# A streaming encoder layer on one core: token rows loaded three at a time and at an earlier gate, and convolution taps ordered behind softmax minima

## The chip, the cores and the metric

The kernel runs on one core of one Trainium2 chip. The metric is the device time of one execution in microseconds (us): 3044.03 us as the median of three runs of the kernel before. The engines of the core work in parallel and in order, each on its own queue: the matmul engine (PE, with its weight loads shown as PEld), the vector engine (DVE), the scalar engine (ACT), GpSimd (POOL), and SyncE (SP), which here issues the DMA transfers. They wait for one another by semaphores.

## The reference

One layer of a streaming encoder, in float32, for a prompt of 2048 tokens and a sample of 64 tokens (2112 in all), model width 1024:

- `h = rms_norm(x, norm1_g) * (1 + sc1) + sh1`, with scales and shifts from a small product of the condition `c`;
- one input projection `z = h @ w_in`, whose columns are a convolution pair (2 x 512), q, k, v (512 each) and two gates (1024 each);
- convolution branch: `u = glu_a * sigmoid(glu_b)`, a causal depthwise convolution of width 31 over the tokens, a LayerNorm over the 512 channels, swish, and a product with `w_conv_out`;
- attention branch: eight heads of 64, q and k normalised, each chunk of 64 tokens reads itself and the eight chunks before, a learned bias by distance, softmax, a product with v and with `w_attn_out`;
- the two are gated, added, projected by `w_o` and added to x; then a second RMS norm and a SwiGLU feed-forward layer of width 2816.

The outputs are the two token arrays and the new convolution, key and value states.

## The kernel before

**Stages.** The first phase (to about 1223 us of the profiled span) computes the input projection, the convolution and the attention in four token blocks: block 0 has the 64 sample tokens and 512 prompt tokens (576 columns), blocks 1 to 3 have 512 each. For each block the stages run in the order q, 0, k, 1, v, 2, 3, g: q, k and v are the attention's products, 0 to 3 are the four 128-channel tiles of the convolution pair, and g is the sixteen gate tiles of 128 columns. The second phase does the merge, the output projection and the feed-forward layer. Every product is made of three matmuls (`mm3`: the high part of the tokens `hh` by the high part of the weights `whi`, `hl` by `whi`, `hh` by `wlo`), so in the profile `ps<-hh,whi`, `ps<-hl,whi` and `ps<-hh,wlo` follow one another. In block 0 the weights are split into `whi` and `wlo` on the way (`wlo<-wst,whi` on DVE or POOL).

**What sets the order.** The program emits the big products in stage order, and between them work from *lanes* of generators: `norm_lane` (token tiles of the next block), `work` (rows of q and k), `attn` (attention heads), `tail` (LayerNorm after the convolution) and `conv` (the convolution's taps, in bursts of four). An object `Stream` adds up an estimated load for each engine; a lane hands on its next piece when the estimated time has come and the engines' estimated backlog is under the lane's room. What is emitted is then given by the framework's scheduler to each engine's queue; the emission order and the dependencies decide, and the queue is fixed when the program is built.

**Token rows.** At gate 11 (`NORM_G`) of a block's g stage the generators of the next block's four prompt tiles are put on `norm_lane`, two at work at a time. Each (`norm_tile`) loads its 128 x 1024 tokens (`x_t`, 512 KB, three buffers), goes on when 8 us of estimated PE time have passed (`X_LAG`), squares and sums them on ACT (`junk<-x_t`), scales them on DVE (`x_t<-x_t,r`), transposes them on PE (`pt<-ident,x_t`, two groups of four), applies scale and shift on DVE (`h<-pt,A,B`) and splits the result into `hh` (ACT) and `hl` (DVE), which the block's products read.

**Taps.** `glu` makes u, the convolution's input for 128 channels, and `convolve` applies the 31 taps to it on DVE: the first is a multiply and add with the bias (`y<-u,wd,cols`), the other thirty are `y<-u,wd,y`, each reading the y of the one before. In block 0 they are 606 columns wide, in the others 512. When a block's taps are done, POOL adds the four channel tiles into `s`, and PE multiplies that by a matrix of ones for the channel means (`pm<-s,ones`): in block 0 first for the 64 sample columns, then for 512.

**Attention.** For each head and each 128 queries PE forms the scores (`sc<-kk,q`), DVE adds the bias and takes a minimum along the row in one custom instruction (`pr<-sc,bias`, called the minimum here; the bias and scale are signed so that it stands for the maximum), ACT takes the exponentials, DVE a reciprocal of the sum (`sm<-sm`). Then PE transposes (`ptp<-ident,pr`), ACT and DVE split (`ph`, `pl<-ptp,ph`) and PE multiplies by the values (`po<-ph,vv`, `po<-pl,vv`). Two score buffers are used in turn; a further score product waits for the minimum of the one two before it, or, in block 0, where two products share a buffer, of the one before. The instruction of the last minimum is kept in `now["least"]`, which nothing reads before the change.

Of the kernel before, what the change touches and what calls it, by code (L numbers as in the profile page):

```python
# [11 lines left out]
ALU = mybir.AluOpType  # L12
# [4 lines left out]
P = 128  # L17
# [15 lines left out]
QB = 512  # L33
# [13 lines left out]
X_LAG = 8000.0  # L47
# [5 lines left out]
SIDE_G = 10  # L53
SPLIT_G = 2
NORM_G = 11
NORM_W = 2
SCORE_ROOM = {"dve": 2500}
TURN_NS = 600.0
# [12 lines left out]
def halves(lo, hi):  # L71
    n = hi - lo
    if n <= 512:
        return [(lo, hi)]
    mid = lo + n // 2
    return [(lo, mid), (mid, hi)]
# [511 lines left out]
def streaming_layer(ctx: ExitStack, tc: tile.TileContext, I, O):  # L588
    nc = tc.nc
    stream = Stream()  # L590
    pe, dve, act, gps = (
        Meter(e, n, stream) for e, n in ((nc.tensor, "pe"), (nc.vector, "dve"), (nc.scalar, "act"), (nc.gpsimd, "pool"))
    )
# [10 lines left out]
    def rows(prompt, sample, t, n):  # L604
        return prompt[t - SMP : t - SMP + n] if t >= SMP else sample[t : t + n]
# [32 lines left out]
    wd = const.tile([P, 4, TAPS], F32, name="wd")  # L638
# [59 lines left out]
    def rsqrt_mean(pool, ssq, n, width, count):  # L698
        t = pool.tile([P, 8], F32, tag="rs_t", bufs=4)
        r = pool.tile([P, 8], F32, tag="rs_r", bufs=4)  # L700
        dve.tensor_scalar(t[:n, :width], ssq, 1.0 / count, EPS, ALU.mult, ALU.add)
        stream.after("pool", "dve")
        gps.tensor_tensor(r[:n, :width], t[:n, :width], mhalf[:n, :width], ALU.pow)
        return r[:n, :width]
# [30 lines left out]
    def temp(name, shape=(P, 512)):  # L735
        return wk.tile(list(shape), F32, tag="t", name=name, bufs=NT)
# [345 lines left out]
    def load_x(t, n, pool, tag, bufs):  # L1082
        x_t = pool.tile([P, D], F32, tag=tag, name="x_t", bufs=bufs)
        nc.sync.dma_start(x_t[:n], rows(x_p, x_s, t, n))
        return x_t

    def square(x_t, n):
# [4 lines left out]
        dve.tensor_tensor(ssq[:n, 0:1], ssq[:n, 0:1], ssq[:n, 1:2], ALU.add)  # L1092
        return rsqrt_mean(wk, ssq[:n, 0:1], n, 1, D)

    def norm_tile(lo, t, free):

        c = slice(t - lo, t - lo + P)
        x_t = load_x(t, P, wa, "x", 3)
        yield stream.load["pe"] + X_LAG
        r = square(x_t, P)  # L1100
        yield stream.when("pool")
        dve.tensor_scalar(x_t, x_t, r, None, ALU.mult)
        yield stream.when("dve") + PE_LAG
        for g in range(2):
            pt = ps_g.tile([P, 4, P], F32, tag="gp", name="pt")
            h = temp("h32", (P, 4, P))
            for k in range(4):
                pe.transpose(pt[:, k], x_t[:, (4 * g + k) * P : (4 * g + k + 1) * P], ident)
            stream.after("dve", "pe")
            for k in range(4):  # L1110
                kk = 4 * g + k
                dve.tensor_scalar(h[:, k], pt[:, k], A1[:, kk, 0:1], B1[:, kk, 0:1], ALU.mult, ALU.add)
            yield stream.when("dve")
            yield lambda: free["columns"] >= c.stop
            f = slice(4 * g, 4 * g + 4)
            act.activation(hh[:, f, c], h, AF.Copy)
            yield stream.when("act")
            dve.tensor_tensor(hl[:, f, c], h, hh[:, f, c].bitcast(F32), ALU.subtract)
# [35 lines left out]
    def kts(t, a=0, b=KT):  # L1154
        return [t[:, k] for k in range(a, b)]
# [29 lines left out]

    now = {"scored": -1, "finished": -1, "bias": None}

    def convolve(u, y, ct, b):
        w = UW if b == 0 else HIST + QB
        n = w - HIST  # L1190
        states = [(cs_s, HIST + SMP)] if b == 0 else [(cs_p, w)] if b == len(PBLOCKS) - 1 else []
        if states:
            yield stream.when("dve") + TURN_LAG
        for rows_, e in states:
            pt = ps_g.tile([P, 512], F32, tag="gp", name="pt")
            pe.transpose(pt[:HIST, :P], u[:, e - HIST : e], ident)
            s = wa.tile([HIST, P], F32, tag="cc", name="cc", bufs=2)
            dve.tensor_scalar(s, pt[:HIST, :P], 0.5, None, ALU.mult)
            stream.at(stream.when("dve"), lambda s=s, rows_=rows_: nc.sync.dma_start(rows_[:, ct * P : (ct + 1) * P], s))
            yield  # L1200
        gps.tensor_copy(hist[:, ct], u[:, w - HIST : w])
        dve.tensor_scalar(y[:, ct, :n], u[:, :n], wd[:, ct, 0:1], bdw[:, ct : ct + 1], ALU.mult, ALU.add)
        for k in range(1, TAPS):
            dve.scalar_tensor_tensor(y[:, ct, :n], u[:, k : k + n], wd[:, ct, k : k + 1], y[:, ct, :n], ALU.mult, ALU.add)
            yield

    def conv_norm(y, c0, n, t0):
# [57 lines left out]
    def gates(b, free):  # L1265

        o = PBLOCKS[b][0]
        w = PBLOCKS[b][1] - o

        def part(g, ws, c0, c1):  # L1270
            ps = columns(*ws, kts(hh), kts(hl), c0, c1)
            t = temp("gate")
            stream.after("act", "pe")
            act.activation(t[:, : c1 - c0], ps[:, : c1 - c0], AF.Tanh, scale=0.5)
            nc.scalar.dma_start(g_d[g // 8, g % 8, :, o + c0 : o + c1], t[:, : c1 - c0])

        def pair(g):
            ws = [W.get(("in", 2560 + g * P, h)) for h in range(2)]
            return [[[w[l][:, k, e * P : e * P + P] for w in ws for k in range(4)] for l in range(2)] for e in range(2)]

        n = 16 - SPLIT_G if b + 1 < len(PBLOCKS) else 16
        for g in range(0, n, 2):
            for e, ws in enumerate(pair(g)):
                for c in halves(0, w):
                    part(g + e, ws, *c)
                if e:
                    W.done()
                    W.done()
                yield g + e
        rest = [ws for g in range(n, 16, 2) for ws in pair(g)]  # L1290
        for c0, c1 in ((0, w // 2), (w // 2, w)):
            for i, ws in enumerate(rest):
                part(n + i, ws, c0, c1)
                if c1 == w and i % 2:
                    W.done()
                    W.done()
            free["columns"] = c1
# [205 lines left out]

    norm_lane, work = Lane({}, wide=NORM_W), Lane({}, wide=3)
    attn = Lane(ATTN, ATTN_NS, wide=2)
# [6 lines left out]
    wa = side.enter_context(tc.tile_pool(name="wa", bufs=1, side="right"))  # L1512
# [11 lines left out]
    for b, stage in ORDER:  # L1524
        lo, hi = PBLOCKS[b]
        if stage == "q":
            free, ahead = {"columns": 0}, {}
            if b + 1 < len(PBLOCKS):
                ahead = {t: norm_tile(hi, t, free) for t, _ in token_tiles(*PBLOCKS[b + 1])}
        if stage == "q" and b == 0:  # L1530
            pass
        elif stage in ("q", "k", "v"):
            qkv(b, "qkv".index(stage), norms)
            if stage == "v":

                def heads(b=b):
                    work.drain()
                    stream.flush()
                    attention(b)
                    if b == 3:  # L1540
                        attn.burst, attn.spacing = 2, 0.0

                stream.at(stream.load["pe"] + HEADS_NS, heads)
        elif stage == "g":
            for g in gates(b, free):
                if g == NORM_G:
                    for gen in ahead.values():
                        norm_lane.add(gen)
                if g == SIDE_G and b == len(PBLOCKS) - 1:
                    work.drain()  # L1550
                    conv.drain()
                    stream.flush()
                    side.close()
                    wc = ctx.enter_context(tc.tile_pool(name="wc", bufs=1, side="right"))
                    cs = tile_chunks(*CBLOCKS[0])[0]
                    src = load_mixed(*cs, 0)
                    first_gates = gate_columns(*cs, 0)
            norms = ahead
        else:
            if b == 0 and stage == 1:  # L1560
                bias_rows()
            if stage == 0:
                conv.drain()
                tail.drain()
                y = wk.tile([P, 4, YW], F32, tag="y", name="y")
            conv.add(convolve(glu(b, stage), y, stage, b))
            if stage == 3:
                if b == 0:
                    tail.add(conv_norm(y, 0, SMP, 0))
                    tail.add(conv_norm(y, SMP + HIST, QB, SMP))  # L1570
                else:
                    tail.add(conv_norm(y, 0, QB, lo))
        for _ in range(MODS.get((b, stage), 0)):
            next(mods)
# [541 lines left out]
```

## Time and profile before

| | us |
|---|---|
| median of three runs (3043.26 to 3046.47) | 3044.03 |
| the profiled execution | 3045.71 |
| its span, first to last instruction | 3043.9 |
| PE busy in the span | 2932.8 |
| DVE, ACT, POOL busy | 1996.2, 1321.8, 984.2 |
| mean granted PE clock | 0.985 |

All lines of the profile are of one execution. An instruction line begins with its start in us from the span's start and its duration (of a group of equal ones the whole), then engine, line, operation, out<-in, shape and count; the brackets hold the idle time of the engine ahead of it and what ended it. All compute instructions are issued through one wrapper, so they carry one line number (L103 before, L104 after the change): they are told apart by the names of tiles and by shapes. A line of a stretch gives its bounds and, for each engine, busy time and number of instructions.

### The profile page before, as it was taken

To read this page: it belongs to the slowest core of one execution; us is meant where nothing else is said; L and a number is where in the kernel's file an instruction comes from. 1 tells how busy PE (TensorE), PEld (TensorE's weight loads), DVE (VectorE), ACT (ScalarE), POOL (GpSimd) and SP (SyncE) were. 2 spreads that over 40 slices of the span, in tenths; PEclk is the share of its full clock that TensorE was granted. 3 is DMA by queue.
4 is the path that set the end of the run, shared out by engine and by line. 5 is a ranking of instruction groups with operands and counts; after the bars stand their busy time and mean duration, and the time that the engine had idled before them with its cause. 6 is when DMAs were issued, how large, how long until landed. Compare 5 with 4: busy or idle time off the path is not lost. (4 is left out here: it accounts for less than half of the span.)

```text
span 3043.9 us, 44749 instructions
## 1 busy us (share of the span) xinstructions
PE 2932.8 (96%) x16259; PEld 2609.7 (86%) x16259; DVE 1996.2 (66%) x3595; ACT 1321.8 (43%) x2371; POOL 984.2 (32%) x617
## 2 busy tenths in 40 slices
PE   7989898999999999989999999999999999999998
PEld 4889776887888888878989889999999898999997
DVE  5896687667956895566666755655666756366567
ACT  3334542563365257463444425534444244333332
POOL 1200120101011102345677433247767341333331
PEclk9999998999999999999999999999999999999999
DMA  9788798877997788886444786455556965355544
GB/s 304 261 278 285 254 298 296 273 246 264 299 289 222 267 270 267 257 278 216 148 144 143 233 283 206 159 164 190 184 194 202 340 213 191 118 167 174 166 161 176
DMA packets 487018, 690.97 MB, mean 227 GB/s; under 512 B 38420, under 2 KB 316808, under 8 KB 486797
## 3 DMA queue, kind: packets, MB, share of 16 engines
q1 hardware_dynamic: 474517, 670.72, 67.2%
q10 hardware_dynamic: 12280, 17.39, 1.6%
q8 instruction: 128, 2.10, 0.3%
q14 instruction: 93, 0.76, 0.1%
HBM read 503.79 MB, written 184.19 MB: 226 GB/s over the span
## 5 line engine op out<-in xcount | busy, mean ns | idle before, releaser
L103 POOL TENSOR_TENSOR wlo<-wst,whi 128x1024 fp32r<-128x1024 f32 (+1 forms) x180 | 401.7, 2238 | 497.6 <-ACT whi L103 452.2
L103 PE MATMUL ps<-t,whi 128*128 128x384 f32 (+1 forms) x2112 | 507.4, 325 | 10.9 <-DVE t L103 5.2
L103 PE MATMUL pd<-whi,hid 128*128 128x512 f32 (+1 forms) x1400 | 450.6, 392 | 3.3 <-DVE acc L103 3.3
L103 ACT ACTIVATE whi<-wst 128x1024 fp32r<-128x1024 f32 (+1 forms) x273 | 266.1, 979 | 356.7 <-PE ps L103 123.4
L103 PE MATMUL ps<-b,whi 128*128 128x384 f32 (+1 forms) x1584 | 381.1, 326 | 11.6 <-DVE pw L103 4.0
L103 PEld LDWEIGHTS ps<-t,whi 128*128 128x128 f32 x2112 | 371.8, 190 | 19.2 <-DVE t L103 6.2
L103 DVE SCALAR_TENSOR_TENSOR y<-u,wd,y 128x512 f32<-128x512 f32 (+1 forms) x480 | 369.2, 773 | 8.2
L103 PE MATMUL ps<-hh,whi 128*128 128x512 f32 (+2 forms) x992 | 364.5, 367 | 1.0 <-DMA whi<-w_din_h 0.8
L103 PE MATMUL ps<-hl,whi 128*128 128x512 f32 (+2 forms) x992 | 346.9, 350 | 0.0
L103 PE MATMUL ps<-hh,wlo 128*128 128x512 f32 (+2 forms) x992 | 346.9, 350 | 0.0
L103 DVE TENSOR_TENSOR acc<-acc,pd 128x512 f32<-128x512 f32 (+1 forms) x440 | 290.7, 684 | 80.5 <-PE pd L103 76.7
L103 PE MATMUL ps<-t,wlo 128*128 128x384 f32 (+1 forms) x1056 | 341.6, 324 | 0.0
L103 PEld LDWEIGHTS pd<-whi,hid 128*128 128x128 f32 (+1 forms) x1400 | 258.4, 185 | 64.4 <-DVE acc L103 6.8
L103 PEld LDWEIGHTS ps<-b,whi 128*128 128x128 f32 x1584 | 277.9, 189 | 14.9 <-DVE pw L103 4.3
L103 PE MATMUL pd<-wlo,hid 128*128 128x512 f32 (+1 forms) x700 | 274.1, 392 | 0.0
L103 PE MATMUL ps<-b,wlo 128*128 128x384 f32 (+1 forms) x792 | 257.4, 325 | 0.0
L103 ACT ACTIVATE pr<-pr,sm 128x640 f32<-128x640 f32 (+3 forms) x272 | 200.1, 747 | 128.1 <-DVE sm L103 126.2
L103 POOL TENSOR_TENSOR r<-t,mhalf 128x1 f32<-128x1 f32 (+3 forms) x68 | 82.2, 1211 | 412.8 <-DVE t L103 369.1
L103 PEld LDWEIGHTS ps<-hh,wlo 128*128 128x128 f32 x992 | 188.2, 190 | 22.5 <-issue 0.4
L103 POOL TENSOR_TENSOR wlo<-wup,whi 128x1024 fp32r<-128x1024 f32 (+1 forms) x64 | 138.2, 2161 | 212.5 <-ACT whi L103 196.7
L103 PEld LDWEIGHTS ps<-hh,whi 128*128 128x128 f32 x992 | 189.1, 191 | 20.0 <-issue 2.7
L103 PEld LDWEIGHTS ps<-hl,whi 128*128 128x128 f32 x992 | 189.1, 191 | 15.5 <-issue 1.7
(215 smaller groups left out, 5719.6 us busy)
## 6 DMA issues: line engine op xcount, KB each, us to landing
whi<-w_din_h SPq DMA_DIRECT2D x72, 512.0 KB, 4.1
wlo<-w_din_l SPq DMA_DIRECT2D x72, 512.0 KB, 7.1
wst<-sum_d SPq DMA_DIRECT2D x131, 256.0 KB, 2.9
wmod<-in_w_ada SPq DMA_DIRECT2D x48, 512.0 KB, 7.2
sum_d<-ws SPq DMA_DIRECT2D x88, 256.0 KB, 2.5
wst<-in_w_ffn_in SPq DMA_DIRECT2D x85, 256.0 KB, 3.5
wst<-in_w_in SPq DMA_DIRECT2D x40, 512.0 KB, 7.4
wst<-in_w_ffn_in SPq DMA_DIRECT2D x37, 512.0 KB, 5.5
```

The lines of the kernel that those rows point to most:

```text
L103: return f(*args, **kw)
```

## The change

Two things are edited.

1. **Token rows.** A small function `ask` loads a tile's rows once and remembers when it may be used. At gate 3 (`ROWS_G`) of a block's g stage the first three tiles of the next block are asked for together; at gate 11 the generators start as before. The fourth tile, which needs a buffer of the three to be free, is asked for from inside the first tile's generator, after its second group of transposes.
2. **Taps.** In blocks 0 and 1 (`b < 2`) a tap that is emitted after a softmax minimum, the first since that minimum, is issued under `tc.issue_after(minimum)`: the scheduler may not put it ahead of that minimum in DVE's queue. No semaphore is added, since both are on one engine. The later taps of the same tile follow, since each reads the y of the one before.

```diff
+ROWS_G = 3
...
+    asked = {}
+
+    def ask(t):
+
+        if t not in asked:
+            asked[t] = load_x(t, P, wa, "x", 3), stream.load["pe"] + X_LAG
+
     def norm_tile(lo, t, free):
 
         c = slice(t - lo, t - lo + P)
-        x_t = load_x(t, P, wa, "x", 3)
-        yield stream.load["pe"] + X_LAG
+        ask(t)
+        x_t, landed = asked.pop(t)
+        yield landed
...
                 pe.transpose(pt[:, k], x_t[:, (4 * g + k) * P : (4 * g + k + 1) * P], ident)
+            if g and t + 3 * P < lo + QB:
+                ask(t + 3 * P)
...
+    def behind(one):
+
+        return tc.issue_after(one.ins) if one is not None else nullcontext()
+
...
         for k in range(1, TAPS):
-            dve.scalar_tensor_tensor(y[:, ct, :n], u[:, k : k + n], wd[:, ct, k : k + 1], y[:, ct, :n], ALU.mult, ALU.add)
+            with behind(now.pop("least", None) if b < 2 else None):
+                dve.scalar_tensor_tensor(y[:, ct, :n], u[:, k : k + n], wd[:, ct, k : k + 1], y[:, ct, :n], ALU.mult, ALU.add)
...
             for g in gates(b, free):
+                if g == ROWS_G:
+                    for t in list(ahead)[:3]:
+                        ask(t)
                 if g == NORM_G:
```

The rows below are those of the engines' queues as built (operation, out<-in, shape, count); ISA rows are the minimum and the read of its result.

DVE's queue in block 1, from the last u of the convolution to the four minima of the first head. Before:

```order
L103 SCALAR_TENSOR_TENSOR u<-tb,ps 128x512
L103 TENSOR_SCALAR y<-u,wd,cols 128x512
L103 COPY R<-pa 128x256
L103 SCALAR_TENSOR_TENSOR y<-u,wd,y 128x512 x4
L103 TENSOR_TENSOR A_173<-pa,cols 128x2x2x2
L103 SCALAR_TENSOR_TENSOR y<-u,wd,y 128x512
L103 TENSOR_TENSOR A_173<-A_173,cols 128x2x2x2
L103 SCALAR_TENSOR_TENSOR y<-u,wd,y 128x512 x15
L103 ISA pr,sm<-sc,bias 128x640
```

And now:

```order
L104 SCALAR_TENSOR_TENSOR u<-tb,ps 128x512
L104 TENSOR_SCALAR y<-u,wd,cols 128x512
L104 COPY R<-pa 128x256
L104 TENSOR_TENSOR A_173<-pa,cols 128x2x2x2
L104 TENSOR_TENSOR A_173<-A_173,cols 128x2x2x2
L104 ISA pr,sm<-sc,bias 128x640
L104 ISA sm 128x1
L104 RECIPROCAL sm<-sm 128x1
L104 ISA pr,sm<-sc,bias 128x640
```

Twenty taps (4, 1 and 15) stood between the u and the first minimum; none does now. In block 0 the corresponding rows are seven taps before and three now, and counted from the program's start 72 and 63.

DVE's queue in block 0, at the head whose last scores (64x320, the sample's) come just before the channel sum of the sample's columns. Before:

```order
L103 TENSOR_TENSOR pl<-ptp,ph 128x512
L103 ISA pr,sm<-sc,bias 64x320
L103 ISA sm 64x1
L103 TENSOR_TENSOR pl<-ptp,ph 128x384
L103 TENSOR_TENSOR pl<-ptp,ph 128x256
L103 TENSOR_TENSOR y<-y,pm 128x64 x4
```

And now:

```order
L104 ISA pr,sm<-sc,bias 64x320
L104 ISA sm 64x1
L104 SCALAR_TENSOR_TENSOR y<-u,wd,y 128x606
L104 TENSOR_TENSOR pl<-ptp,ph 128x256
L104 SCALAR_TENSOR_TENSOR y<-u,wd,y 128x606
L104 RECIPROCAL sm<-sm 64x1
L104 TENSOR_TENSOR wlo<-wst,whi 128x1024
L104 SCALAR_TENSOR_TENSOR y<-u,wd,y 128x606
L104 TENSOR_TENSOR wlo<-wst,whi 128x1024
L104 SCALAR_TENSOR_TENSOR y<-u,wd,y 128x606 x4
L104 TENSOR_TENSOR y<-y,pm 128x64 x4
```

Block 0's last seven taps now stand behind this minimum; before, all taps of block 0 were issued ahead of it. On PE, the product `pm<-s,ones 128x64` stands six `ps` and six `po` products after these scores.

PE's queue in block 3 at its first head (`q_10842`). Before, the first two of four score products:

```order
L103 MATMUL sc<-kk,q_10842 128x320 x4
L103 MATMUL ps<-hh,whi 128x512
L103 MATMUL ps<-hl,whi 128x512
L103 MATMUL ps<-hh,wlo 128x512
L103 MATMUL ps<-hh,whi 128x512
L103 MATMUL ps<-hl,whi 128x512
L103 MATMUL ps<-hh,wlo 128x512
L103 MATMUL sc<-kk,q_10842 128x320 x4
```

And now:

```order
L104 MATMUL ps<-hh,whi 128x512
L104 MATMUL ps<-hl,whi 128x512
L104 MATMUL ps<-hh,wlo 128x512
L104 MATMUL sc<-kk,q_10842 128x320 x16
L104 MATMUL ptp<-ident,pr 128x128 x2
```

The four score products stand in one run, with no other product between them, though the diff names neither block 3 nor the scores. On SP the token rows of block 1, which were two single loads and two later ones, are now one row of three (`DMA x_t<-in_x_prompt 128x1024 x3`) 35 places earlier in the queue, and a single load.

## The prediction

> **What bounds the kernel now.** I read the engines' shares first, then the idle stretches of the matmul engine (PE) in order of time with what ended each, then, at each of them, the vector engine (DVE) and the scalar engine (ACT) at the same moment, and last the granted clock of those stretches. The first line is the page's, the others are of the view by stretches (us; PE, PEld, DVE, ACT and POOL busy; granted clock; DMA share; GB/s).
>
> ```profile
> PE 2932.8 (96%) x16259; PEld 2609.7 (86%) x16259; DVE 1996.2 (66%) x3595; ACT 1321.8 (43%) x2371; POOL 984.2 (32%) x617
> ...
> 189.30:202.95 13.65, 7.96 (x27) 6.29 (x28) 12.22 (x25) 4.43 (x12) 0.00 (x0) 0.50 0.34 120
> 359.97:370.20 10.23, 7.32 (x19) 4.84 (x20) 6.54 (x20) 6.08 (x12) 3.74 (x3) 0.50 1.05 280
> 496.50:513.57 17.07, 7.11 (x23) 5.69 (x24) 15.00 (x29) 6.11 (x12) 0.00 (x0) 0.50 0.54 193
> 950.48:953.88 3.40, 1.77 (x7) 1.19 (x8) 3.34 (x10) 0.63 (x1) 1.18 (x1) 1.00 0.20 50
> 953.89:957.29 3.40, 3.40 (x10) 2.64 (x9) 2.99 (x8) 1.55 (x3) 0.27 (x1) 0.50 0.00 0
> 957.31:960.70 3.39, 3.39 (x22) 2.86 (x21) 1.98 (x3) 2.07 (x4) 1.35 (x1) 1.00 0.00 0
> ```
>
> PE is busy for 2932.8 of 3043.9 us, so only its idle time (111 us) and its half-speed time can be won. Three of the worst places are the ones that the change touches. A wait costs twice: in 950.48 to 953.88 PE was idle for 1.63 of 3.40 us, and the next 3.40 us, though full, ran at clock 0.50; after it the clock is 1.00 again. So I charge half of PE's busy time in a half-clock stretch: 7.96/2 = 4.0, 7.32/2 = 3.7 and 7.11/2 = 3.6 us. The waits (start, length; in brackets the idle time before and what ended it):
>
> ```profile
> 188.43 0.41 PE L103 MATMUL sc<-kk,q 128*128 128x128 f32 x2 [2.10 <-DMA kk<-k_d]
> 194.21 0.80 PE L103 MATMUL sc<-kk,q 128*128 128x256 f32 x2 [5.37 <-DVE sm L103]
> 355.73 0.47 PE L103 MATMUL po<-ph,vv 128*128 128x512 f32 x1 [1.28 <-DMA vv<-v_d]
> 360.04 1.97 PE L103 MATMUL pt<-ident,x_t 128*128 128x128 f32 x8 [3.61 <-DVE x_t L103]
> 365.62 0.79 PE L103 MATMUL ps<-whi,hh 128*128 128x512 f32 x1 [2.33 <-ACT hh L103]
> 504.61 1.43 PE L103 MATMUL sc<-kk,q 128*128 128x320 f32 x4 [10.18 <-DVE sm L103]
> 506.97 1.44 PE L103 MATMUL sc<-kk,q 128*128 128x320 f32 x4 [0.93 <-DVE sm L103]
> ```
>
> At 194.21 and 504.61 scores wait for DVE's minimum of the scores before. What DVE did until then (first a stretch: its busy time, the granted clock, DMA share, GB/s):
>
> ```profile
> 150.00:200.00 50.00, 48.09 (x71) 0.89 0.80 268
> ...
> 187.78 6.16 DVE L103 SCALAR_TENSOR_TENSOR y<-u,wd,y 128x606 f32<-128x606 f32 x7
> 193.86 0.28 DVE L103 CUSTOM_DVE_ANT_0 pr<-sc,bias 128x128 f32<-128x128 f32 x1
> ...
> 492.04 11.78 DVE L103 SCALAR_TENSOR_TENSOR y<-u,wd,y 128x512 f32<-128x512 f32 x15
> 503.73 0.82 DVE L103 CUSTOM_DVE_ANT_0 pr<-sc,bias 128x640 f32<-128x640 f32 x1
> ```
>
> Seven taps at 0.88 us (6.16/7) and fifteen at 0.785 (11.78/15) stood ahead of the minimum, and DVE was busy for 48.09 of the 50 us around the first head, so a tap less anywhere ahead of it counts in full. At 360.04 the cause is a late load:
>
> ```profile
> 351.25 0.50 SPq L1084 DMA_DIRECT2D x_t<-in_x_prompt  x1
> 353.10 0.70 SPq L1084 DMA_DIRECT2D x_t<-in_x_prompt  x1
> ...
> 356.86 0.63 ACT L103 ACTIVATE junk<-x_t 128x512 f32<-128x512 f32 x1 [2.48 <-DMA x_t<-in_x_prompt]
> 361.66 0.63 ACT L103 ACTIVATE junk<-x_t 128x512 f32<-128x512 f32 x1 [3.46 <-DMA x_t<-in_x_prompt]
> ```
>
> The third and fourth token tiles are asked for at 351 and 353 us, and ACT's squares of them wait at 356.86 and 361.66.
>
> **Gains.** First head of block 0: in the whole of DVE's order nine taps fewer stand ahead of the first minimum (63 instead of 72). Nine times 0.88 is 7.9 us, more than the wait of 5.37; what remains is the minimum itself, about 0.4. Gain 5.0. The wait of 2.10 for kk stays, and with what follows it is more idle time than the 1.63 us above, so one half-clock stretch of 3.4 us stays too (1.5 of the 4.0 us, the short waits between the four score products taking most of the rest). I take 6 us, 5 to 7.5.
>
> First head of block 1: twenty taps fewer ahead of the minimum, 20 x 0.785 = 15.7 us, more than the 10.18. Of the wait about 0.9 (minimum and its read) stays, and the two waits of 0.9 behind it, since two score buffers alternate with a minimum of 0.82. So 9.3 is won and nearly all the 3.6 of half clock; 1 off because the displaced taps meet the head's later work. I take 12, 10 to 13.5.
>
> Token rows, block 0 to 1: with three tiles in place by the fourth gate, the waits 1.28, 3.61 and 2.33 go with their half clock: 7.2 + 3.7 = 10.9. The fourth tile is still loaded inside the first tile's norm, and the transposes' chain through DVE and ACT (about 3 us) stands at another place among the products; 1 us off. I take 10, 8 to 12. The other blocks show no such row and get nothing. The three loads are 1.5 MB; at the 277 GB/s of the row below they take 5.7 us of the queues, ahead of weight slabs and the next heads' rows. I cost this at nothing: the same bytes are only moved, the DMA engines are 0.83 busy there, and weights are asked for ahead of use. Without that cover it is the third rival.
>
> **Losses.** The displaced taps return later, one behind each minimum, each holding up DVE's queue. First the rows for DVE's cover in block 0, then those at the place where its taps are needed (the sum for LayerNorm, pm).
>
> ```profile
> 250.00:290.00 40.00, 38.94 (x283) 37.23 (x282) 20.97 (x57) 22.49 (x54) 0.45 (x2) 1.00 0.83 277
> ...
> 256.41 1.21 DVE L103 TENSOR_TENSOR wlo<-wst,whi 128x1024 fp32r<-128x1024 f32 x1
> 257.61 1.72 DVE L103 SCALAR_TENSOR_TENSOR y<-u,wd,y 128x606 f32<-128x606 f32 x2
> 259.47 0.30 POOL L103 TENSOR_TENSOR s<-s,y 128x64 f32<-128x64 f32 x1 [33.78 <-DVE y L103]
> ...
> 286.00 0.30 PE L103 MATMUL ps<-hl,whi 128*128 128x288 f32 x1
> 286.13 0.29 PE L103 MATMUL ps<-hh,wlo 128*128 128x288 f32 x1
> 287.10 0.45 PE L103 MATMUL sc<-kk,q 128*64 128x320 f32 x2
> 287.57 0.69 DVE L103 TENSOR_TENSOR pl<-ptp,ph 128x512 fp32r<-128x512 f32 x1 [5.67 <-ACT ph L103]
> 288.18 0.47 DVE L103 CUSTOM_DVE_ANT_0 pr<-sc,bias 64x320 f32<-64x320 f32 x1
> 288.34 0.33 PE L103 MATMUL pm<-s,ones 128*128 128x64 f32 x2
> 290.56 0.39 PE L103 MATMUL po<-ph,vv 128*128 128x512 f32 x1
> 290.79 0.39 PE L103 MATMUL po<-pl,vv 128*128 128x512 f32 x1
> ```
>
> Before, the last tap ends at 259.4 and pm runs unhindered at 288.34: 29 us of slack, while DVE is about half busy (20.97 of 40). In the changed order seven taps, two wlo and one pl of 256 columns stand between the minimum of the 64x320 scores and the end of the taps: 7 x 0.86 + 2 x 1.21 + 0.4 (0.69 for 512) + 0.47 for the minimum = 9.3 us, then POOL's add, 0.30. PE has only six products of 288 columns (0.13 apart by 286.00 and 286.13) and six po between those scores and pm: 6 x 0.13 + 1.0 (0.23 apart for 512 columns, less for the shorter ones) = 1.8 us. PE waits 9.6 - 1.8 = 7.8. Idle that long, it then runs at half clock until a full stretch is over: 1.7 to 3.4 us, I take 2.5. Sum 10.5; between 6 (DVE reaches the minimum 3 us earlier relative to PE, and one half-clock stretch) and 14 (the minimum 2 late, two stretches). Queued behind these taps on DVE are the subtraction of pm and the next pl, which PE needs only later.
>
> The head before it: eight taps, one wlo and four small ones, 8.8 us by the same rows, stand between two minima where PE has 34 products of 288 columns and small ones, 5.3 us. The minimum is 3.5 late, PE has 1.2 us of products before the next score write of the same tile: 2.5 lost (0 to 4). The second sum of block 0 and that of block 1 (eleven taps of 0.785 and POOL's adds, 10 us against 11 us of PE work) together 2 (0 to 5).
>
> Block 3, which the diff doesn't name, also moves: the four score products of its first head now stand in one run.
>
> ```profile
> 1047.71 5.47 DVE L103 SCALAR_TENSOR_TENSOR y<-u,wd,y 128x512 f32<-128x512 f32 x7
> 1058.39 0.74 PE L103 MATMUL sc<-kk,q 128*128 128x320 f32 x4
> 1059.17 0.82 DVE L103 CUSTOM_DVE_ANT_0 pr<-sc,bias 128x640 f32<-128x640 f32 x1 [2.36 <-PE sc L103]
> 1060.35 0.74 PE L103 MATMUL sc<-kk,q 128*128 128x320 f32 x4
> 1063.85 0.68 DVE L103 SCALAR_TENSOR_TENSOR u<-tb,ps 128x512 f32<-128x512 f32 x1
> ```
>
> Before, 1.96 us lie between two score products, filled with products, and DVE waits for PE. Now a u, a first tap and seven taps (0.68 + about 0.6 + 5.47 = 6.7 us) precede the minimum, against some 5.4 us of PE's last product group (24 at 0.23); the third score product waits 1.6, the fourth 1.7 (a minimum and two taps less 0.6 of scores), the transposes 1.05: 4.35, and half a stretch of half clock, 1.7. I take 6, 4 to 8.5.
>
> A rule against the row: the Trainium skill, "TensorE: Matmul & The Clock Gate", section "What's actually happening", lets the clock fall only after at least one idle window of about 3.4 us. By it the short waits of block 3 would cost no clock and the sum would be 1.7 us better, about 3035. The row at 953.89 disagrees (half clock after 1.63 us idle of 3.40), so I go by the row.
>
> **Sum.** 6 + 12 + 10 - 10.5 - 2.5 - 2 - 6 = +7 us. The profiled execution took 3045.7 us (span 3043.9), 1.7 above the median of 3044.03; taken off the median, 7 us give 3037. By the terms' ends together, one in three of them unlucky, 3030 to 3044.
>
> **Rivals.** *DVE gets ahead* (0.25): each wait of PE lets DVE catch up, and it starts block 0's heads nine taps lighter; the sums' waits then shrink to half and block 3's burst costs its lower end, losses of 10 instead of 21: 3026. For it: DVE's 20.97 of 40 us. Against: an in-order queue holds a tap that waits for a minimum even when DVE has nothing else.
>
> *The sum's wait grows* (0.18, slower): the same queue now holds taps behind work that waits for ACT; the row at 287.57 shows such a wait, 5.67. Two of them between the first head and pm delay the last tap by 11 us more and cost another stretch of half clock, 3: 7 us slower in all, 3051. It decides from the point where PE waits over 15 us for pm. Against: those waits exist because DVE is early, and here it is late.
>
> *The loads collide* (0.09): the 5.7 us of rows delay the next head's kk or vv, as 355.73 shows for two loads (1.28). At two gates 2 us and 1.5 of clock each, 7 in all: 3044. That the change does nothing is excluded: both orders show the taps and loads moved.
>
> **Chances.** Forecast 0.48, of which 0.28 lies below 3038, 0.18 within 0.2% (6 us, what a measurement of this kernel can tell from none) and 0.02 above. With 0.25 faster; 0.16 of 0.18 slower; loads 0.07 same, 0.02 slower: faster 0.53, same 0.27, slower 0.20. Range 3023 to 3050: the fast case whole and the slow one's lower half.
>
> **What would show it.** Right: no PE wait over 1.5 us at the first heads of blocks 0 (but kk) and 1, none at the pt of block 1's token tiles, and clock 1.00 in 496 to 514 shifted; a wait of about 8 us for POOL's s before block 0's first pm, ended by a tap on DVE; three short waits at block 3's first head. Wrong: if pm waits under 3 us (3026), over 15 (3051), or if kk, vv or whi show as the releasers of new waits.

## The result, and the profile after

The changed kernel takes 3028.25 us (median of five runs, 3026.45 to 3034.51); the kernel before, beside it, 3043.77 (3041.86 to 3046.47). The ratio is 0.9958 with a 95% interval of 0.9945 to 0.9971: 0.3 to 0.55% faster, some 13 us (the two medians lie 15.5 apart). A second comparison gave 0.9956 (0.9942 to 0.9971). The forecast was 3037 in a range of 3023 to 3050, 7 us faster: the direction and the range hold, the gain was about twice as large.

The profiled execution of the changed kernel took 3034.51 us, the longest of its five, with a span of 3032.7, 11.2 us under that of before; that of the second comparison has a span of 3030.3, 13.6 us under it. First the page's line of engine shares, then the idle stretches of PE at the places of the forecast (view of the timeline; in brackets the idle time before and what ended it).

```profile
PE 2932.0 (97%) x16259; PEld 2605.6 (86%) x16259; DVE 1995.8 (66%) x3595; ACT 1320.1 (44%) x2371; POOL 982.7 (32%) x617
...
189.52 0.41 PE L104 MATMUL sc<-kk,q 128*128 128x128 f32 x2 [1.98 <-DMA kk<-k_d]
191.08 0.80 PE L104 MATMUL sc<-kk,q 128*128 128x256 f32 x2 [1.15 <-DVE sm L104]
...
270.17 0.39 PE L104 MATMUL ptp<-ident,pr 64*128 64x64 f32 x3 [2.06 <-ACT pr L104]
290.32 0.47 PE L104 MATMUL sc<-kk,q 128*64 128x320 f32 x2 [0.75 <-DMA kk<-k_d]
301.81 0.69 PE L104 MATMUL pm<-s,ones 128*128 128x64 f32 x2 [8.95 <-POOL s L104]
338.99 0.47 PE L104 MATMUL sc<-kk,q 128*64 128x320 f32 x2 [2.11 <-DMA kk<-k_d]
439.28 0.41 PE L104 MATMUL sc<-kk,q 128*128 128x128 f32 x2 [1.40 <-DMA kk<-k_d]
...
498.52 0.85 PE L104 MATMUL sc<-kk,q 128*128 128x320 f32 x4 [0.92 <-DVE sm L104]
500.40 0.86 PE L104 MATMUL sc<-kk,q 128*128 128x320 f32 x4 [1.04 <-DVE sm L104]
568.50 1.12 PE L104 MATMUL pm<-s,ones 128*128 128x512 f32 x2 [1.31 <-POOL s L104]
...
1049.74 0.85 PE L104 MATMUL sc<-kk,q 128*128 128x320 f32 x4 [0.71 <-DMA kk<-k_d]
1051.52 0.85 PE L104 MATMUL sc<-kk,q 128*128 128x320 f32 x4 [0.93 <-DVE sm L104]
1053.72 1.07 PE L104 MATMUL sc<-kk,q 128*128 128x320 f32 x4 [1.34 <-DVE sm L104]
1055.71 1.43 PE L104 MATMUL sc<-kk,q 128*128 128x320 f32 x4 [0.93 <-DVE sm L104]
```

PE's busy time is that of before (2932.0 against 2932.8); what went is idle time. The waits of 5.37, 10.18, 3.61 and 2.33 us are gone or down to about 1 us, and six places wait that did not, or hardly: the transposes at 270, the sum pm at 301.81, two heads whose kk comes late (338.99 and 439.28; before, the wait at the second was 0.35), the sum of block 1 at 568.50, and block 3's first head. What DVE and POOL do ahead of pm:

```profile
289.62 0.84 DVE L104 SCALAR_TENSOR_TENSOR y<-u,wd,y 128x606 f32<-128x606 f32 x1
290.83 0.48 DVE L104 CUSTOM_DVE_ANT_0 pr<-sc,bias 64x320 f32<-64x320 f32 x1 [0.38 <-PE sc L104]
291.25 0.84 DVE L104 SCALAR_TENSOR_TENSOR y<-u,wd,y 128x606 f32<-128x606 f32 x1
292.01 0.41 DVE L104 TENSOR_TENSOR pl<-ptp,ph 128x256 fp32r<-128x256 f32 x1
292.34 0.83 DVE L104 SCALAR_TENSOR_TENSOR y<-u,wd,y 128x606 f32<-128x606 f32 x1
294.70 0.15 DVE L104 RECIPROCAL sm<-sm 64x1 f32<-64x1 f32 x1 [1.52 <-ACT pr L104]
294.78 1.22 DVE L104 TENSOR_TENSOR wlo<-wst,whi 128x1024 fp32r<-128x1024 f32 x1
295.92 0.84 DVE L104 SCALAR_TENSOR_TENSOR y<-u,wd,y 128x606 f32<-128x606 f32 x1
296.68 1.22 DVE L104 TENSOR_TENSOR wlo<-wst,whi 128x1024 fp32r<-128x1024 f32 x1
297.82 3.50 DVE L104 SCALAR_TENSOR_TENSOR y<-u,wd,y 128x606 f32<-128x606 f32 x4
...
301.46 0.30 POOL L104 TENSOR_TENSOR s<-s,y 128x64 f32<-128x64 f32 x1 [59.03 <-DVE y L104]
```

It is the chain that the forecast summed: from the minimum at 290.83 to the last tap's end at 301.3 are 10.5 us (9.3 forecast). The difference is 1.52 us in which a reciprocal waits for ACT, with the wlo and the taps behind it in DVE's queue. The clock (view by stretches, columns as before):

```profile
296.42:306.65 10.23, 4.84 (x21) 4.84 (x22) 5.61 (x11) 1.01 (x5) 1.09 (x4) 0.50 1.04 310
501.22:504.63 3.41, 3.41 (x13) 2.92 (x12) 1.34 (x4) 1.73 (x4) 0.00 (x0) 0.50 1.03 382
1054.18:1061.00 6.82, 5.89 (x22) 4.80 (x21) 5.43 (x14) 5.16 (x10) 0.00 (x0) 0.50 0.85 250
```

After pm PE is busy for 4.84 us at half clock, which costs 2.4 (2.5 forecast); at block 1's first head one half-clock stretch is left of the five, after waits of 0.92 and 1.04 (in the 3.41 us ahead of it, 497.81 to 501.22, PE is idle for 1.75).

**Where the time went.** The program has the same `ps` products in all versions. The table gives, for stretches of the profile before, how much later (+) or earlier (-) the same number of `ps` products was reached, end of the stretch less its start. It is worked out from the start times of the `ps` rows of each trace, and good to 1 us, 2 at the start of the program; small work that moves across a border shows on both sides of it, above all at 1040. The versions are those of the experiments below.

| stretch (us, before) | place | change | change again | rows only | taps only | taps block 1 | two heads |
|---|---|---|---|---|---|---|---|
| 180-205 | first head, block 0 | -4.4 | -2.8 | +0.3 | -3.8 | +1.3 | -3.3 |
| 262-285 | third sample head | +3.4 | +2.2 | +5.1 | +0.4 | +3.6 | +4.6 |
| 285-300 | first pm | +12.5 | +11.5 | 0.0 | +8.3 | 0.0 | 0.0 |
| 340-372 | start of block 1 | -8.9 | -8.9 | -7.1 | -5.6 | -6.3 | -7.7 |
| 492-520 | first head, block 1 | -12.2 | -13.6 | -0.1 | -9.9 | -12.2 | -13.5 |
| 520-600 | sums, block 1 | +2.7 | +2.8 | -0.7 | +2.9 | +2.8 | +2.7 |
| 690-740 | start of block 2 | -3.3 | -3.3 | -3.3 | 0.0 | -3.3 | -3.3 |
| 860-1040 | start of block 3 | -7.2 | -6.7 | -7.0 | -0.9 | -6.8 | -7.2 |
| 1040-1110 | first head, block 3 | +7.0 | +7.0 | +6.9 | -0.5 | +6.6 | +6.8 |
| to 3000 | whole | -11.2 | -13.6 | -10.2 | -11.0 | -20.6 | -27.5 |

### The profile page after: what moved, and what is told of

Read it like the earlier page. It is cut to its first block, busy times and chain, and to the rows that moved or that the text cites. A ratio compares the mean times of both kernels' runs of the same rounds, so it can differ in the third digit from the quotient of the medians.

```text
span 3032.7 us, 44756 instructions
## 1 busy us (share of the span) xinstructions
PE 2932.0 (97%) x16259; PEld 2605.6 (86%) x16259; DVE 1995.8 (66%) x3595; ACT 1320.1 (44%) x2371; POOL 982.7 (32%) x617
## 5 line engine op out<-in xcount | busy, mean ns | idle before, releaser
L104 PE MATMUL ps<-b,whi 128*128 128x384 f32 (+1 forms) x1584 | 381.2, 326 | 11.2 <-DVE pw L104 4.0
L104 ACT ACTIVATE pr<-pr,sm 128x640 f32<-128x640 f32 (+2 forms) x272 | 199.9, 746 | 104.4 <-DVE sm L104 102.3
```

Of the source, the lines that this page charges most:

```text
L104: return f(*args, **kw)
```

## The experiments

Each was timed beside the kernel before on the same chip. A ratio is from all executions of a comparison; a span is that of the one profiled execution, which can lie some us off the median.

### The token rows alone

```diff
-            with behind(now.pop("least", None) if b < 2 else None):
+            with behind(now.pop("least", None) if b < 0 else None):
```

> The token rows as in the change, the taps without any new order. Theory (the prediction's terms add up): rows +10 us at the start of block 1, -6 us for block 3's first head, whose four score products stand in one run in this order too; so 4 us faster than before, about 3040, with the 10.18 us wait at block 1's first head still there and no wait for POOL's s before block 0's first pm. Rival 1 (the rows carry most of the change's 15.5 us, also at the starts of blocks 2 and 3): 3030 to 3033. Rival 2 (the rows bring nothing): 3044 or above.

Measured: 3033.62 against 3041.0 us, ratio 0.9976 (0.9966 to 0.9986), 7 us faster; 4 were expected by the theory, 11 to 14 by the first rival (3030 to 3033, put against the 3044 of before), and the second (nothing) falls. As expected the wait at block 1's first head is there and none at pm. Not expected is the third sample head of block 0. First two rows of the kernel before, then four of this run:

```profile
265.64 0.45 PE L103 MATMUL sc<-kk,q 128*64 128x320 f32 x2
269.07 0.39 PE L103 MATMUL ptp<-ident,pr 64*128 64x64 f32 x3
...
249.57 1.29 SPq L1085 DMA_DIRECT2D x_t<-in_x_prompt  x3
270.17 0.45 PE L104 MATMUL sc<-kk,q 128*64 128x320 f32 x2
272.71 0.39 PE L104 MATMUL ptp<-ident,pr 64*128 64x64 f32 x3 [2.09 <-ACT pr L104]
...
502.86 1.44 PE L104 MATMUL sc<-kk,q 128*128 128x320 f32 x4 [9.40 <-DVE sm L104]
```

The two matmuls of the scores at 270.17 stand in this order right ahead of the transposes that need their softmax; before, 23 other matmuls lay between the two, and the rows' loads are all that differs. PE waits 2.09 us and the clock falls (0.50 from 274.23 to 281.06): 5.1 us in the table. And the rows bring 3.3 and 7.0 us at the starts of blocks 2 and 3, where the forecast gave them nothing.

### The taps alone

```diff
-                if g == ROWS_G:
-                    for t in list(ahead)[:3]:
-                        ask(t)
...
-            if g and t + 3 * P < lo + QB:
-                ask(t + 3 * P)
```

> The taps as in the change, the token rows loaded as before. Theory: +6 and +12 us at the first heads of blocks 0 and 1, -10.5, -2.5 and -2 for pm and the heads before it; block 3's four score products are apart again in this order, so no loss there: 3 us faster than before, about 3041. Rival (the gap between the forecast 7 and the measured 15.5 lies in the taps): 3033. The wait before block 0's first pm is to be about 9 us, as in the changed kernel (8.95).

Measured: 3034.07 against 3041.0 us, 0.9971 (0.9960 to 0.9982), 9 us: more than the 3 of the theory, nearer to the rival's 11. Its rows:

```profile
294.16 0.69 PE L104 MATMUL pm<-s,ones 128*128 128x64 f32 x2 [5.55 <-POOL s L104]
...
361.89 0.48 PE L104 MATMUL sc<-kk,q 128*64 128x320 f32 x2 [1.52 <-DMA kk<-k_d]
364.81 0.80 PE L104 MATMUL ps<-whi,hh 128*128 128x512 f32 x1 [2.44 <-ACT hh L104]
```

pm waits 5.55 and not 9: from the minimum to the last tap DVE takes 8.3 us and not 10.5, with six taps in place of seven and no wait for ACT's pr. And the start of block 1 gets 5.6 us shorter though its rows are loaded as before. The wait of 3.61 us for x_t ended with a transfer. Its two loads are issued at 350.28 and 352.49 (before: 351.25 and 353.10), and PE comes there 5 us later, so part of pm's wait is no loss: it is taken off a wait for data that come at about the same time anyway. The two parts together (0.9958) bring less than the product of the two (0.9976 times 0.9971 is 0.9947), though the intervals don't exclude that they are equal. In the table they fall short of their sum at two places: by 3.8 us at the start of block 1, which both shorten, and by 4.2 at pm, where the change waits longer than the taps alone.

### The taps in the second block only

```diff
-            with behind(now.pop("least", None) if b < 2 else None):
+            with behind(now.pop("least", None) if b == 1 else None):
```

> The change with the taps' order in the second block only (b == 1), rows as in the change. Theory: block 0 loses the 6 us of its first head but is also free of pm's wait and what goes with it (13 us): 7 us faster than the changed kernel, about 3021, and the 5.37 us wait at 194 us is back. Rival (pm's wait only holds time that would be lost at a later place of block 0): within 2 us of the changed kernel, 3026 to 3030.

Measured: 3024.08 against 3041.0 us, 0.9942 (0.9929 to 0.9955); the span is 3023.3, 9.4 under that of the changed kernel. The theory's 7 fits better than the rival's none by the span; by the ratios (0.9942 against 0.9956 to 0.9958) it is 4 to 5 us, between the two, and the intervals overlap. pm runs without a wait (0.0 in the table), and the first head of block 0 has its long wait back.

### The taps in block 0 until the second head is scored

```diff
-            with behind(now.pop("least", None) if b < 2 else None):
+            with behind(now.pop("least", None) if b == 1 or b == 0 and now["scored"] <= 1 else None):
```

> The change with the taps' order in block 0 only until the second head is scored; in this order 63 taps stand ahead of block 0's first minimum as in the changed kernel, and the last tap stands ahead of the fourth head's first minimum, so that neither of the two late heads nor pm has taps between it and its minimum. Theory: the changed kernel without the losses at pm (8.95 us measured there, 10.5 with the clock) and the head before it (2.5): 13 us faster, about 3015. Rival (the taps are only shifted, DVE is the bound of block 0, and PE waits for its minima earlier instead): gain under 4 us, 3024 to 3028.

Measured: 3021.17 against 3041.0 us, 0.9932 (0.9918 to 0.9945); span 3016.4, the changed kernel's less 16.3, or 13.9 less than that of its second profile. The theory's 13 holds by the spans, but these overstate it: the change's profiled execution was the slowest of its five (6.3 over their median), this version's lay 3 under its median. By the ratios it is about 7, half of the theory and more than the rival's 4. Its rows:

```profile
191.03 0.79 PE L104 MATMUL sc<-kk,q 128*128 128x256 f32 x2 [1.24 <-DVE sm L104]
271.12 0.39 PE L104 MATMUL ptp<-ident,pr 64*128 64x64 f32 x3 [3.23 <-ACT pr L104]
290.27 0.33 PE L104 MATMUL pm<-s,ones 128*128 128x64 f32 x2
```

The short wait of the first head stays short (1.24), pm does not wait, and the table has 0.0 where the change has +12.5. So the taps that were held back to the very last minima of block 0 cost those 12 us at pm, and bought nothing that shows elsewhere (the first head of block 0 gains 3.3 without them, 4.4 and 2.8 with them). This version beats the kernel before by 0.7%; against the change the medians say 7 to 8 us, with intervals that just touch (up to 0.9945 here, from 0.9942 there).

One wait that neither the kernel before nor the change has is at the second sum of block 0:

```profile
358.64 1.13 PE L104 MATMUL pm<-s,ones 128*128 128x512 f32 x2 [2.25 <-POOL s L104]
```

POOL's last add for that sum stands at 357.32, right behind its work on a token tile (`r<-t,mhalf`), for whose input POOL had waited until 356.81. The rows-only run waits 2.72 us there and the kernel before not at all, so it is a second cost of block 1's early rows, already taken off in the table's -7.7.

### The changed kernel once more

Nothing is edited here.

> The changed kernel once more, beside the three that follow. It tells how far its 15.5 us hold on another chip. Theory: its profiled execution, 11.2 us shorter in span than that of before, is the better measure, since its terms add up to that, 0.9958 to 0.9965 of before; rival (the profiled execution was a slow one): 0.9950 or less. The wait before block 0's first pm is 8 to 9 us again, and the waits of block 3's first head add up to about 4.

Measured: 3029.19 against 3041.11 us, 0.9956 (0.9942 to 0.9971), just outside the theory's range (0.9958 to 0.9965) and nearer to it than to the rival's 0.9950 or less; the interval holds both. Its rows:

```profile
299.17 0.69 PE L104 MATMUL pm<-s,ones 128*128 128x64 f32 x2 [7.75 <-POOL s L104]
...
1050.61 0.85 PE L104 MATMUL sc<-kk,q 128*128 128x320 f32 x4 [0.93 <-DVE sm L104]
1052.80 1.34 PE L104 MATMUL sc<-kk,q 128*128 128x320 f32 x4 [1.35 <-DVE sm L104]
```

pm waits 7.75 (8.95 in the first, 8 to 9 expected), as the forecast's sum had it (7.8). With 0.85 for kk and 0.92 at the last product, the waits at block 3's first head are 4.05 in all, as expected.

### The rows of block 1 at gate 1

The edit is made on the version with two heads.

```diff
-                if g == ROWS_G:
+                if g == (1, ROWS_G, ROWS_G, 99)[b]:
```

> The version with taps ordered in block 0 until the second head is scored, and the rows of block 1 asked for at gate 1 instead of gate 3 (blocks 2 and 3 at gate 3 as in the change). In this order the scores of block 0's third sample head stand 29 matmuls ahead of the transposes that need them, as before the change (25), and not 2. Theory (the loads' place moves those scores, and PE waits for the exponentials, 3.23 us plus half clock): 4 us faster than that version. Rival (the 1.5 MB of rows delay the kk of that head wherever they are put): no difference, and the wait shows at the kk load.

Measured: 3024.56 against 3041.11 us, 0.9945 (0.9933 to 0.9957): not 4 us faster, rather 4 slower than the version it is made from, though the intervals overlap. The loss at 262 to 285 is gone as the theory said (0.0), but 6.5 us are lost between 250 and 262 instead, where the two-heads version has -0.2. Two rows of PE and four of DVE there:

```profile
251.91 0.50 PE L104 MATMUL sc<-kk,q 128*128 128x256 f32 x2 [1.54 <-DVE sm L104]
257.76 2.00 PE L104 MATMUL ptp<-ident,pr 128*128 128x128 f32 x7 [1.62 <-ACT pr L104]
...
243.47 6.15 DVE L104 SCALAR_TENSOR_TENSOR y<-u,wd,y 128x606 f32<-128x606 f32 x7
249.54 1.22 DVE L104 TENSOR_TENSOR wlo<-wst,whi 128x1024 fp32r<-128x1024 f32 x1
250.68 0.84 DVE L104 SCALAR_TENSOR_TENSOR y<-u,wd,y 128x606 f32<-128x606 f32 x1
251.55 0.29 DVE L104 CUSTOM_DVE_ANT_0 pr<-sc,bias 128x128 f32<-128x128 f32 x1
```

The scores stood ready at 249.8; between the write of `part_l` and their minimum DVE's queue holds seven taps, a wlo and one more tap, in the two-heads version three taps and no wlo. So the rival, the 1.5 MB delaying a kk, falls: no kk is waited for. The place of the loads in the program changes what the plan emits around them, and both places tried so far, gates 3 and 1, have some head whose scores or minimum come late for it.

### Two tiles ahead for block 3

Again on the version with two heads.

```diff
-                    for t in list(ahead)[:3]:
+                    for t in list(ahead)[: 2 if b == 2 else 3]:
```

> The version with taps ordered in block 0 until the second head is scored, and only two of the three tiles of block 3's rows asked for ahead. In this order block 3's first four score products have other products between them again, 15 matmuls ahead of the transposes as before the change, not 0. Theory (the run of four costs 3.9 us of waits and half clock): 5 to 7 us faster than that version. Rival (the third tile's late load costs as much at the start of block 3, where the three tiles bring 6 us): no difference.

Measured: 3018.76 against 3041.11 us, 0.9930 (0.9917 to 0.9943), as the version it is made from (0.9932). The rival holds. The loss at block 3's first head is gone (1040 to 1110: +0.3 in place of +6.8), and so is the gain at its start (860 to 1040: -0.4 in place of -7.2), where a wait for hh stands that neither the kernel before nor the change has there (it is of the kind of before's 2.33 at 365.62):

```profile
929.32 0.79 PE L104 MATMUL ps<-whi,hh 128*128 128x512 f32 x1 [3.13 <-ACT hh L104]
```

### Both edits together

```diff
-                if g == ROWS_G:
-                    for t in list(ahead)[:3]:
+                if g == (1, ROWS_G, ROWS_G, 99)[b]:
+                    for t in list(ahead)[: 2 if b == 2 else 3]:
```

> Taps ordered in block 0 until the second head is scored, rows of block 1 at gate 1, two tiles ahead for block 3: both edits of the two versions before together. If the terms add up: 4 + 6 = 10 us under the version with the taps alone, some 31 us under before, 0.990. If the waits only change places: at most 4 under it, 0.992.

Measured: 3027.34 against 3041.11 us, 0.9952 (0.9939 to 0.9964), about 6 us slower than the two-heads version. Both expectations miss; it is what the two edits before give together, one a loss, one nothing or a little less. The traces have the waits of the gate-1 version at 250 to 262 (+6.5) and the late start of block 3 of the two-tile version (+1.2 from 860 to 1040, where the two-heads version has -7.2).

### Two tiles late for block 1

On the version with two heads: for block 1 two tiles at gate 9, for block 2 three at gate 3, for block 3 two at gates 6 and 8.

```diff
-                if g == ROWS_G:
-                    for t in list(ahead)[:3]:
+                for t, at_ in zip(ahead, ((9, 9), (3, 3, 3), (6, 8), ())[b]):
+                    if g == at_:
                         ask(t)
```

> Taps ordered in block 0 until the second head is scored; rows of block 1: two tiles at gate 9 instead of three at gate 3; of block 2: three at gate 3; of block 3: two, at gates 6 and 8. In this order no scores stand right ahead of the transposes that need them, neither in block 0 (31 and 13 matmuls at the third and fifth sample heads) nor in block 3 (15). Theory (the loss of 4 to 5 us at the third sample head is the price of the early loads, and two tiles by gate 11 are nearly as good as three): 4 us faster than the version with the taps alone, 0.992 or less. Rival (the third tile's late load costs what the early loads save): no difference, 0.993.

Measured: 3026.47 against 3042.54 us, 0.9946 (0.9933 to 0.9958), some 4 us slower than with three tiles at gate 3: both expectations miss. The loss at the third sample head is nearly gone (262 to 285: +0.7), but the third tile's late load costs more than the early loads do: +2.3 from 355 to 372, where the two-heads version has -8.2. There PE waits 4.39 and 2.78 us for x_t. Block 3 comes out as with two tiles ahead: no loss of 7 at its first head (+1.2) and no gain at its start (-0.2).

### Early rows from block 2 on

On the version with two heads, with block 1's rows loaded as before the change.

```diff
-                if g == ROWS_G:
-                    for t in list(ahead)[:3]:
+                for t, at_ in zip(ahead, ((), (3, 3, 3), (3, 3, 3), ())[b]):
+                    if g == at_:
                         ask(t)
```

> Taps ordered in block 0 until the second head is scored; the rows of block 1 loaded as before the change, those of blocks 2 and 3 at gate 3 as in the change. Theory: the loss of 4.6 us at block 0's third sample head and of 2.2 at its fifth goes, the gain of 8 at the start of block 1 goes too: 1 us slower than the version with the taps alone, 0.9935. Rival (the early rows of block 1 are worth their 10 us net, as the prediction had it): 10 us slower, 0.9965.

Measured: 3021.72 against 3042.54 us, 0.9933 (0.9920 to 0.9947), against 0.9932 with block 1's early rows. The theory (1 us) holds, the rival (10 us) falls. The waits at block 1's token tiles are back:

```profile
357.23 1.12 PE L104 MATMUL pt<-ident,x_t 128*128 128x128 f32 x4 [5.43 <-DVE x_t L104]
361.04 1.12 PE L104 MATMUL pt<-ident,x_t 128*128 128x128 f32 x4 [2.69 <-DVE x_t L104]
365.52 0.79 PE L104 MATMUL ps<-whi,hh 128*128 128x512 f32 x1 [1.98 <-ACT hh L104]
```

and the loss at 262 to 285 is gone (+0.1); between 250 and 262 there is one of 1.9 in its stead, as in the version before this one (+1.8). The third and fourth tile are asked for together here, at 348.17, where the kernel before asks at 351.25 and 353.10. By the spans (3022.3 against 3016.4) the early rows of block 1 are still worth some 6 us, by the ratios nothing; of the 6, 5.4 are the profiled executions' distance from their medians (2.4 over here, 3.0 under there). So the early rows of block 1 don't bring the 9 us that they win at the start of block 1 taken alone.

## Why the prediction was right, and where it was not

*First head of block 1* (12, 10 to 13.5): right, 12.2 and 13.6, and seen with the taps in that block alone (12.2). The clock is not 1.00 throughout, as the signs had it: one stretch at 0.50 is left in the first profile.

*First head of block 0* (6, 5 to 7.5): less than its range, 2.8 to 4.4. The wait for kk stayed as said, the first minimum's wait is 1.15 and not the 0.4 that was put.

*Token rows, start of block 1* (10, 8 to 12): right by its own stretch, 8.9. But the same loads cost 2.2 to 5.1 us at the third sample head of block 0. The step that failed there is "I cost this at nothing". It is not the third rival, loads that collide: in the rows-only run no kk or weight is waited for there. (The forecast had named kk as the releaser of new waits among the signs of being wrong, and the change has two of them later, 2.11 at 338.99 and 1.40 at 439.28. The three tiles are asked for some 90 us before the first, and rows alone wait 0.48 at the second and not at the first; what delays these kk stays open.) The loads' emission moved those scores straight ahead of their transposes in PE's queue; I had looked at where the rows stood in SP's queue, not at what their earlier emission did to PE's.

*pm* (10.5, with 2.5 at the head before it, 13 together): the mechanism is right, with 12.5 and 11.5 in the table, and 0.0 in both versions that leave those taps ahead. Waits of 8.95 and 7.75 against 7.8; the half clock 2.4 against 2.5. The head before it has no wait over 0.3 us where 2.5 were put, so that the two together come so near to 13 is luck: pm took more than its 10.5 and the head nothing. *Sums* (2): 2.7 in block 1.

*First head of block 3* (6, 4 to 8.5): right in its size, 7.0, and rows alone bring it, taps alone do not. The waits are 0.71, 0.93, 1.34 and 0.93, in all 3.9 against 4.35, but not where they were put: the first is for kk, the second, third and fourth score products wait, and the transposes do not. The two score buffers that the forecast and the text before it speak of are not there in blocks 1 to 3: a product of 640 columns takes the whole score tile and waits for the minimum just before it (the minimum at 1050.64 and its read end at 1051.46, the next product starts at 1051.52). The half clock costs 2.9 (half of 5.89) and not 1.7.

*The step that made the forecast half too small*: "The other blocks show no such row and get nothing." They got 3.3 us at the start of block 2 and about 7 at that of block 3. Rows of the profile before do show waits there; they are shorter and lie apart:

```profile
670.18 0.51 PE L103 MATMUL ps<-whi,hh 128*128 128x512 f32 x1 [1.13 <-ACT hh L103]
678.98 0.50 PE L103 MATMUL ps<-whi,hh 128*128 128x512 f32 x1 [0.59 <-ACT hh L103]
753.49 0.71 PE L103 MATMUL pa<-sel,R 128*128 128x128 f32 x4 [2.36 <-DVE R L103]
952.11 0.82 PE L103 MATMUL sc<-kk,q 128*128 128x320 f32 x4 [1.79 <-DMA kk<-k_d]
1030.12 0.27 PE L103 MATMUL pt<-ident,u 128*30 128x128 f32 x1 [1.10 <-DVE u L103]
```

The row at 952.11 is the very one after which the forecast took its half-clock stretch (1.7 us), and it did not ask whether the change would remove it. All of these are gone in the changed kernel and with rows alone, where between 640 and 1045 us only one wait over 0.4 us is left (0.92, at 734.48 and 739.29), and all are there with the taps alone (the 2.36 as 1.27); so it is the rows that remove them. The table puts the gain of block 2 in the stretch behind its first rows, since small work moves across the border. With these 10 us in and the 3 of the third sample head out, the sum is 14 us; 13 were measured.

*Rivals*: that DVE gets ahead (3026) is not what happened, though the time fell close to it: the waits came at their size. The growing wait at pm (3051) did not come; one wait for ACT joined the taps (1.52 us), not two of 5.67. On the clock, going by the row was right: after block 3's waits of 0.93 and 1.34, none near a whole idle stretch of 3.4 us, the granted clock is 0.50 in 1054.18 to 1061.00, and also in 501.22 to 504.63 after 0.92 and 1.04. The Trainium skill, "TensorE: Matmul & The Clock Gate", section "What's actually happening", puts the fall after an idle window of about 3.4 us; these rows differ from it.

Left open: the stretches of the table are of one execution each, and how far they hold for the median is not shown; the version with two heads is 14 to 16 us ahead of the changed kernel by the spans, some 7 by the medians. And that the early rows of block 1 bring so little net was seen at three places of the loads only (gates 1, 3 and 9); a place that costs nothing was not found.

## What to carry to other kernels

An order edge that moves work behind a late instruction should end where its gain ends: held to the first two heads in block 0, the same edge kept its gains at the first heads (3 and 13 us) and was rid of the loss of 12 us at the sum that needed the last held-back piece. Find the consumer of the last displaced piece and count what now stands between the two on each engine. When loads are moved in a program whose order is planned, look at what the plan does to the matmul engine's queue, in every repetition of the place and not only where the profile has its longest wait; and a wait for data that would come at the same time anyway gives back part of what was lost ahead of it.

## What the runs showed of the hardware that was not expected

A stall ahead of a wait for a transfer is partly free: with the taps alone PE lost 8.3 us at pm, and the start of block 1 got 5.6 us shorter, above all because the waits of 1.28 for vv and 3.61 for x_t went. Two short waits of about 1 us each (0.92 and 1.04; 1.75 us idle in 3.41) were enough for a stretch of 3.41 us at clock 0.50; the forecast had seen this for a single wait of 1.79 only. It does not always follow: in the two-heads version PE is idle for 1.85 of the 3.41 us from 357.01, and the clock stays at 1.00 behind them. And a DVE queue that is held by order alone takes on waits for other engines: 1.52 us for ACT's pr in the middle of block 0's last taps.
